# Attention of two mixers in one written TensorE order, with scaling and weight casts on GpSimd

## The chip, the cores and the metric

The kernel runs on one core of a Trainium2 chip. The metric is the device time of one execution in microseconds. The kernel before has a median of 1093.54 us in three runs (1093.34 to 1095.23).

The engines are called TensorE (PE in the rows, with PEld for its weight loads), VectorE (DVE), ScalarE (ACT), GpSimd (POOL) and SyncE (SP, which issues the loads from HBM).

## The reference

256 tokens of width 1024 go through two layers. Each layer is a half-step gated FFN, a token mixer, a second half-step FFN and a gated embedding, each with an RMS norm before and behind it. The first layer's mixer is A (8 heads in three dilation groups, mixed by their softmax denominators), the second layer's is B (16 query heads on 4 key/value heads, a band of 128 tokens to either side, a sink logit per head). All is float32.

```python
for i in range(DEPTH):
    g = norm_g[i]
    h = h + 0.5 * rms_norm(swiglu(rms_norm(h, g[0]), ffn_wi[i, 0], ffn_wo[i, 0]), g[1])
    hn = rms_norm(h, g[2])
    if mixer == 0:
        y = dilated_mixer(hn, a_wqkv[j], a_wo[j], cos, sin)
    elif mixer == 1:
        y = window_gqa_mixer(hn, b_wqkv[j], b_wo[j], b_sink[j], cos, sin)
    h = h + rms_norm(y, g[3])
    h = h + 0.5 * rms_norm(swiglu(rms_norm(h, g[4]), ffn_wi[i, 1], ffn_wo[i, 1]), g[5])
    ...
```

In both mixers the projections of h give Q, K and V; Q and K are rotated; scores are masked and turned into probabilities; these weigh V; and the output weights (`a_wo`, `b_wo`) project the result.

## The kernel before

The tokens are two tiles of 128 (`t` 0 and 1), held in `h`. Every large product is made of three passes over hi and lo halves (`PASSES`, line 34): `weight` (line 75) loads a 128x1024 tile into a buffer of `raws`, ScalarE casts the hi half (line 87), and VectorE subtracts for the lo half in two pieces (line 90). The pairs lie in `wts`, nine buffers, which the projections of a mixer, its output weights and the next FFN share.

`proj` (line 181) makes one 128x512 projection of a token tile: 24 matmuls of 512 columns into a bank of `ps_a` (two banks), with a call `mid` after the first half. `mixer_a` runs nine blocks of 512 columns (`kind` 0 is Q, 1 is K, 2 is V; `g` is the dilation group), in the order V0, V1, Q0, K0, Q1, K1, Q2, K2, V2, each for both token tiles. A Q or K block is scaled out of PSUM on ScalarE, rotated by four VectorE steps (`rope_`, lines 303 to 306), and its transposition (`heads_T`, four transposes and copies) is put off in `pend` until `flush` is called, which is the default `mid` of the next projection. `mixer_b` runs a K/V block and two Q blocks in the same manner.

Attention goes over eight units, a unit being two heads (A) or two pairs of heads (B) of one token tile: `units` has four for `t` 0, then four for `t` 1.

- `scores` makes 12 matmuls into two banks of `ps_y` (four banks), and `soft` turns each bank into probabilities: a fused mask-add and minimum on VectorE (lines 396, 543), the exponential with its sum on ScalarE (lines 397, 546), a reciprocal (398, 548) and a scaling on VectorE (399, 550). In B each bank holds two heads, so there are two of each but the reciprocal, and a copy of the sink logits (line 541).
- `trans` transposes the probabilities, 4 + 4 transposes into two banks of `ps_t` (two banks), which ScalarE copies to `w2` (line 338).
- `values` makes 16 matmuls into one bank of `ps_a` and splits the result into halves.

`attend` (line 445) goes over the units with two units of scores ahead (`AHEAD`): `score(n + 2)`, `trans(n + 1)`, `values(n)`, and after the fifth unit `finish(0)`, the output projection and norm of token tile 0 (24 matmuls of 512 columns in A, 48 in B). Behind the loop come the transposes of the new activations of tile 0 (`res[0].fin()`) and `finish(1)`; then the next FFN starts.

What sets the order: the kernel is written in program order, and a scheduler orders each engine's instructions by that order and by when it expects their inputs. `tc.manual_schedule` keeps the written order on the engines it names. Before, it encloses in the mixers only the inside of `scores` and of `values`: their matmuls keep their order, but others may come between them. DMAs of weights all go out on SP's queue in the scheduler's order.

## Time and profile before

| | |
|---|---|
| median of three runs | 1093.54 us |
| profiled execution, its own time | 1094.63 us |
| its span, first to last instruction | 1092.9 us |
| TensorE busy | 98% of the span |
| VectorE, ScalarE, GpSimd busy | 64%, 52%, 0% |
| mean granted TensorE clock | 0.99 |

Busy time counts an instruction from its start to its modelled end. TensorE's matmuls are pipelined, so a row's length is that of a run of them including the last one's end, and what a run costs is read from start to start of the rows. The idle time in brackets stands before a row, with what released it.

### The profile page before, as it was taken

Reading aid. Unit: us, or ns where it says so; the run is one execution under the profiler, and the core shown is the slowest. Engines: PE = TensorE matmul, PEld = TensorE weight load, DVE = VectorE, ACT = ScalarE, POOL = GpSimd, SP = SyncE. Lnnn points to the kernel's source line nnn. Section 1 sums busy time; section 2 is a strip of 40 time slices with the busy share of each in tenths; the row PEclk is TensorE's granted clock in tenths of the full one; section 3 lists DMA queues with packets and bytes.
Section 4 is the critical chain, followed back from the end, with each engine's and each line's share of the span. In section 5 each row is a group of like instructions: output and inputs, shape, how many; then the busy total and the mean of one; then the engine's idle time right before and its main releaser. Section 6 shows DMA issues by size and latency. Waiting matters only on the chain.

```text
span 1092.9 us, 14763 instructions
## 1 busy us (share of the span) xinstructions
PE 1066.1 (98%) x5110; PEld 862.5 (79%) x5110; DVE 694.8 (64%) x1523; ACT 570.6 (52%) x896; POOL 0.7 (0%) x6
## 2 busy tenths in 40 slices
PE   7999999999999999999999999999998999999996
PEld 6888888788877888888887888887866888888885
DVE  6765454865666855576588654655975875557465
ACT  5644343655565645454456444544675665446343
POOL 0000000000000000000000000000000000000000
PEclk8999999999999999999999999999999999999998
DMA  8865655565540575576544756655660565567601
GB/s 268 294 199 176 204 182 165 174 221 164 174 135 30 165 229 187 161 246 205 163 138 154 233 170 195 193 162 167 178 170 1 158 214 180 171 211 241 202 1 39
DMA packets 130235, 189.04 MB, mean 173 GB/s; under 512 B 9440, under 2 KB 100320, under 8 KB 130160
## 3 DMA queue, kind: packets, MB, share of 16 engines
q1 hardware_dynamic: 130160, 188.10, 54.8%
q8 instruction: 40, 0.66, 0.2%
q14 instruction: 35, 0.29, 0.1%
HBM read 187.02 MB, written 1.05 MB: 172 GB/s over the span
## 4 chain that ended last, share of the span: by engine, by line
PE 93%; DVE 3%; ACT 2%; DMA 1%; issue 1%; SPq 1%; DVEq 0%; ACTq 0%
PE psa L193 54%; PE psy L204 29%; PE pst L240 2%; PE pst L336 2%; PE psa L414 1%; PE psa L630 1%; PE psy L325 1%; PE pst L146 1%; PE psa L568 1%; PE pst L316 1%; DMA raw<-in_ffn_wi_dram 1%; ACT w L87 1%; DVE w L90 1%; PE psa L187 1%; ACT w2t L338 0%
## 5 line engine op out<-in xcount | busy, mean ns | idle before, releaser
L193 PE MATMUL psa<-w,hgT 128*128 128x512 f32 x2664 | 632.7, 393 | 0.5 <-ACT m4t L375 0.5
L193 PEld LDWEIGHTS psa<-w,hgT 128*128 128x128 f32 x2664 | 494.9, 188 | 103.3 <-ACT m4t L375 0.9
L90 DVE TENSOR_TENSOR w<-raw,w 128x512 fp32r<-128x512 f32 x672 | 435.7, 687 | 174.6 <-ACT w L87 165.1
L87 ACT CAST w<-raw 128x1024 fp32r<-128x1024 f32 (+1 forms) x340 | 352.7, 1042 | 196.2 <-issue 82.3
L204 PE MATMUL psy<-w,w2t 128*128 128x512 f32 x1056 | 260.7, 399 | 2.6 <-ACT w2t L72 2.5
L204 PEld LDWEIGHTS psy<-w,w2t 128*128 128x128 f32 x1056 | 194.4, 188 | 47.8 <-ACT w2t L72 5.4
L231 ACT ACTIVATE w2t<-psa,small 128x256 f32<-128x256 f32 x88 | 41.7, 474 | 158.8 <-PE psa L193 154.5
L232 DVE SCALAR_TENSOR_TENSOR w2t<-psa,small,w2t 128x256 f32<-128x256 f32 x88 | 42.3, 481 | 115.0 <-ACT w2t L231 115.0
L73 DVE TENSOR_TENSOR w2t<-pst,w2t 128x256 fp32r<-128x256 f32 x88 | 36.5, 415 | 9.3 <-ACT w2t L72 9.3
L72 ACT CAST w2t<-pst 128x256 fp32r<-128x256 f32 x88 | 32.1, 364 | 10.1 <-PE pst L240 10.0
L204 PE MATMUL psy<-w,m4t 128*128 128x512 f32 x144 | 37.3, 402 | 0.0
L72 ACT CAST hgT<-w2t 128x512 fp32r<-128x512 f32 x32 | 19.4, 620 | 32.2 <-DVE w2t L148 32.0
L240 PE MATMUL pst<-ident,w2t 128*128 128x128 f32 x176 | 33.5, 271 | 1.5 <-DVE w2t L232 1.5
L240 PEld LDWEIGHTS pst<-ident,w2t 128*128 128x128 f32 x176 | 24.4, 139 | 13.2 <-issue 1.8
L204 PEld LDWEIGHTS psy<-w,m4t 128*128 128x128 f32 x144 | 25.9, 188 | 6.3 <-issue 1.2
L148 DVE TENSOR_TENSOR w2t<-pst,gcol 128x512 f32<-128x512 f32 x32 | 21.2, 685 | 10.9 <-PE pst L146 10.7
L336 PE MATMUL pst<-ident,w2t 128*128 128x128 f32 x128 | 21.4, 292 | 4.4 <-DVE w2t L550 4.3
L204 PE MATMUL psy<-w,hgT 128*128 128x512 f32 x96 | 23.4, 392 | 0.0
L336 PEld LDWEIGHTS pst<-ident,w2t 128*128 128x128 f32 x128 | 14.2, 144 | 11.3 <-issue 8.2
L114 ACT ACTIVATE w2t<-psy 128x512 f32<-128x512 f32 x24 | 14.2, 593 | 16.7 <-DVE w2t L166 16.6
L171 DVE SCALAR_TENSOR_TENSOR h<-w2t,small,h 128x512 f32<-128x512 f32 x32 | 22.6, 748 | 0.4
L204 PE MATMUL psy<-m4t,hgT 128*128 128x512 f32 x96 | 22.6, 389 | 0.0
(88 smaller groups left out, 551.7 us busy)
## 6 DMA issues: line engine op xcount, KB each, us to landing
raw<-in_ffn_wi_dram SPq DMA_DIRECT2D x352, 256.0 KB, 4.1
raw<-in_ffn_wo_dram SPq DMA_DIRECT2D x88, 512.0 KB, 4.9
raw<-in_a_wqkv_dram SPq DMA_DIRECT2D x36, 512.0 KB, 4.6
raw<-in_ple_gate_dram SPq DMA_DIRECT2D x16, 512.0 KB, 3.8
raw<-in_b_wqkv_dram SPq DMA_DIRECT2D x12, 512.0 KB, 4.0
gb<-in_norm_g_dram SPq DMA_DIRECT2D x8, 512.0 KB, 4.9
raw<-in_b_wo_dram SPq DMA_DIRECT2D x16, 256.0 KB, 5.7
raw<-in_a_wo_dram SPq DMA_DIRECT2D x4, 512.0 KB, 4.7
```

The source lines that it names most:

```text
L72: nc.scalar.copy(dst_hi, src)
L73: nc.vector.tensor_tensor(dst_lo, src, dst_hi.bitcast(F32), ALU.subtract)
L87: nc.scalar.copy(w[0][:, i:i + step], raw[:, i:i + step])
L90: nc.vector.tensor_tensor(w[1][:, c], raw[:, c], w[0][:, c].bitcast(F32), ALU.subtract)
L148: nc.vector.tensor_tensor(hg, pt.rearrange("p (k q) -> p k q", k=4), gcol[:, 4 * q:4 * q + 4, self.row].unsqueeze(2).broadcast_to([P, 4, P ...
L171: nc.vector.scalar_tensor_tensor(h[t][:, s], yg[i], r, h[t][:, s], ALU.mult, ALU.add)
L193: nc.tensor.matmul(ps, lhs(a, xh, 2 * c + k), ws[c][wh][:, k * 512:(k + 1) * 512], start=(c == 0 and k == 0 and n == 0), stop=(c == 3 and ...
L204: nc.tensor.matmul(y[half], lhsf(k, xh), ws[k][wh][:, half * 512:(half + 1) * 512], start=(first and k == 0 and i == 0), stop=(last and k ...
L231: nc.scalar.activation(su[:, 0, :], ps[:, 0:256], AF.Silu, scale=acts[t].rstd)
L232: nc.vector.scalar_tensor_tensor(su[:, 1, :], ps[:, 256:512], acts[t].rstd, su[:, 0, :], ALU.mult, ALU.mult)
L240: nc.tensor.transpose(pt[:, f * P:(f + 1) * P], su[:, 1, f * P:(f + 1) * P], ident)
L336: nc.tensor.transpose(pt[:, i * P:(i + 1) * P], sm_of(a), ident)
```

## The change

TensorE's order is written out for the whole of `attend`. A function `lead` of each mixer does the last projections together with the first scores and transposes: in A, the blocks V1 and V2 are moved behind all Q and K blocks, and scores 0 to 2 and the transposes of units 0 and 1 stand between their four projections; in B, the same stands around the second Q block, with the transposes of that block's heads (`flush`) right behind its last projection. The loop then goes `values(n)`, `score(n + 3)`, (`finish(0)` after the fifth unit), `trans(n + 2)`. The hi halves of the output weights are cast by GpSimd, the scaling of the probabilities and B's copy of the sink logits go from VectorE to GpSimd, one of B's two copies of transposed probabilities goes from ScalarE to VectorE, and the pool `w2` has 14 buffers instead of 12.

```diff
--- before.py
+++ after.py
@@ -23,13 +23,13 @@
 RAWS = 5
 SPLIT_A = False
 M4 = 11
+W2 = 14
 PREP = 6
 E_AT = None
 GATE_AT = 8
 GATE_N = 4
 FA = 5
 FB = 5
-AHEAD = 2
 WARM = 9
 PASSES = ((0, 0), (0, 1), (1, 0))
 
@@ -45,7 +45,7 @@
     wts = pool("wts", 9)
     hgs = pool("hgs", 1)
     m4 = pool("m4", M4)
-    w2 = pool("w2", 12)
+    w2 = pool("w2", W2)
     ps_y = pool("ps_y", 4, space=bass.MemoryType.PSUM)
     ps_a = pool("ps_a", 2, space=bass.MemoryType.PSUM)
     ps_t = pool("ps_t", 2, space=bass.MemoryType.PSUM)
@@ -72,7 +72,7 @@
         nc.scalar.copy(dst_hi, src)
         nc.vector.tensor_tensor(dst_lo, src, dst_hi.bitcast(F32), ALU.subtract)
 
-    def weight(loads, later=False, big=False):
+    def weight(loads, later=False, big=False, pool_hi=False):
         raw = raws.tile([P, 1024], F32, name="raw", tag="raw")
         if big:
             w = [m4_tile([P, 1024], F32R) for _ in range(2)]
@@ -84,7 +84,10 @@
 
         def cast(step):
             for i in range(0, 1024, step):
-                nc.scalar.copy(w[0][:, i:i + step], raw[:, i:i + step])
+                if pool_hi:
+                    nc.gpsimd.tensor_copy(w[0][:, i:i + step], raw[:, i:i + step])
+                else:
+                    nc.scalar.copy(w[0][:, i:i + step], raw[:, i:i + step])
             for i in range(0, 1024, LO):
                 c = slice(i, i + LO)
                 nc.vector.tensor_tensor(w[1][:, c], raw[:, c], w[0][:, c].bitcast(F32), ALU.subtract)
@@ -102,8 +105,8 @@
             (lambda r, i=i: r.rearrange("p (kt f) -> p kt f", kt=2)[:, :, i * wd:(i + 1) * wd],
              v[:, :, c0:c0 + wd]) for i, c0 in enumerate(cols)], later)
 
-    def weight_rows(src, k, big=False):
-        return weight([(lambda r: r, src[k * P:(k + 1) * P, :])], big=big)
+    def weight_rows(src, k, big=False, pool_hi=False):
+        return weight([(lambda r: r, src[k * P:(k + 1) * P, :])], big=big, pool_hi=pool_hi)
 
     def inv_rms(parts, factor):
         k = 256.0 / (3.0 * factor)
@@ -330,12 +333,16 @@
     def pv_out(o_ps, oT, slot):
         split(oT[:, 0, slot, :], oT[:, 1, slot, :], o_ps[:, 0:P])
 
-    def transpose_p(sm_of, kts):
+    def transpose_p(sm_of, kts, dve=False):
         pt = bank("t")
         for i, a in enumerate(kts):
             nc.tensor.transpose(pt[:, i * P:(i + 1) * P], sm_of(a), ident)
         pT = w2_tile([P, 4, P])
-        nc.scalar.copy(pT, pt.rearrange("p (n q) -> p n q", n=4))
+        v = pt.rearrange("p (n q) -> p n q", n=4)
+        if dve:
+            nc.vector.tensor_copy(pT, v)
+        else:
+            nc.scalar.copy(pT, v)
         return pT
 
     def out_proj(t, oTs, ws, y):
@@ -396,7 +403,7 @@
             nc.vector.tensor_tensor_reduce(sm, s, msk[:, t, :], 1.0, 3e38, ALU.add, ALU.min, accum_out=mn)
             nc.scalar.activation(sm, sm, AF.Exp, scale=-1.0, bias=mn, accum_out=den)
             nc.vector.reciprocal(rd, den)
-            nc.vector.tensor_scalar(sm, sm, rd, None, ALU.mult)
+            nc.gpsimd.tensor_scalar(sm, sm, rd, None, ALU.mult)
             return sm
 
         oT, pTs = {}, {}
@@ -419,17 +426,14 @@
 
         b0 = block(2, 0)
         b0(0)
-        b1 = block(2, 1)
+        b1 = block(0, 0)
         b1(0, acts[1].fin)
         b0(1)
         b1(1)
-        for g in range(3):
-            for kind in range(2):
-                b = block(kind, g)
-                b(0)
-                b(1)
-        b = block(2, 2)
-        b(0)
+        for kind, g in ((1, 0), (0, 1), (1, 1), (0, 2), (1, 2)):
+            b = block(kind, g)
+            b(0)
+            b(1)
         sms = {}
         units = [(t, pr) for t in range(2) for pr in range(4)]
 
@@ -437,17 +441,25 @@
             if n < len(units):
                 sms[units[n]] = scores(*units[n])
 
-        b(1, lambda: score(0))
-        return attend(units, score, trans, values, 1,
-                      [lambda k=k: weight_rows(a_wo[0], k) for k in range(4)],
+        b1, b2 = block(2, 1), block(2, 2)
+
+        def lead():
+            b1(0)
+            score(0)
+            b1(1)
+            score(1)
+            b2(0)
+            trans(*units[0])
+            score(2)
+            b2(1)
+            trans(*units[1])
+
+        return attend(units, score, trans, values, lead,
+                      [lambda k=k: weight_rows(a_wo[0], k, pool_hi=True) for k in range(4)],
                       lambda t: [oT[t]], gb, row)
 
-    def attend(units, score, trans, values, done, wload, oTs, gb, row, flush=nothing):
-        ahead = AHEAD
-        for n in range(done, ahead):
-            score(n)
-        trans(*units[0])
-        res, ws = [], []
+    def attend(units, score, trans, values, lead, wload, oTs, gb, row):
+        res, ws, y0 = [], [], []
 
         def finish(t):
             if not ws:
@@ -456,15 +468,15 @@
             out_proj(t, oTs(t), ws, y)
             res.append(boundary(t, y, gb, 1.0, row))
 
-        for n, u in enumerate(units):
-            score(n + ahead)
-            if n == 0:
-                flush()
-            if n + 1 < len(units):
-                trans(*units[n + 1])
-            values(*u)
-            if n == 4:
-                finish(0)
+        with tc.manual_schedule(engines={E.PE}):
+            lead()
+            for n, u in enumerate(units):
+                values(*u)
+                score(n + 3)
+                if n == 4:
+                    finish(0)
+                if n + 2 < len(units):
+                    trans(*units[n + 2])
         res[0].fin()
         finish(1)
         return res
@@ -538,7 +550,7 @@
             mn = stat.tile([P, 2], F32, name="pair", tag="pair", bufs=12)
             den = stat.tile([P, 2], F32, name="pair", tag="pair", bufs=12)
             rd = stat.tile([P, 2], F32, name="pair", tag="pair", bufs=12)
-            nc.vector.tensor_copy(sm[:, :, 256], nsk[:, hd0:hd0 + 2])
+            nc.gpsimd.tensor_copy(sm[:, :, 256], nsk[:, hd0:hd0 + 2])
             for i in range(2):
                 nc.vector.tensor_tensor_reduce(sm[:, i, 0:256], s[:, i * 256:(i + 1) * 256], msk[:, t, 0:256], 1.0,
                                                nsk[:, hd0 + i:hd0 + i + 1], ALU.add, ALU.min,
@@ -547,14 +559,14 @@
                                      accum_out=den[:, i:i + 1])
             nc.vector.reciprocal(rd, den)
             for i in range(2):
-                nc.vector.tensor_scalar(sm[:, i, 0:256], sm[:, i, 0:256], rd[:, i:i + 1], None, ALU.mult)
+                nc.gpsimd.tensor_scalar(sm[:, i, 0:256], sm[:, i, 0:256], rd[:, i:i + 1], None, ALU.mult)
             return sm
 
         oT, pTs = {}, {}
 
         def trans(t, pr):
-            pTs[t, pr] = [transpose_p(lambda n: sm[:, n // 2, (n % 2) * P:(n % 2 + 1) * P], range(4))
-                          for sm in sms.pop((t, pr))]
+            pTs[t, pr] = [transpose_p(lambda n: sm[:, n // 2, (n % 2) * P:(n % 2 + 1) * P], range(4), u == 1)
+                          for u, sm in enumerate(sms.pop((t, pr)))]
 
         def values(t, pr):
             a, ih = pr // 2, pr % 2
@@ -578,7 +590,7 @@
             a, i = divmod(k, 4)
             r0 = (8 * a + i) * DH
             return weight([(lambda r, u=u: r[64 * u:64 * u + 64, :], b_wo[0, r0 + 256 * u:r0 + 256 * u + 64, :])
-                           for u in range(2)])
+                           for u in range(2)], pool_hi=True)
 
         b0 = kv_block()
         b0(0)
@@ -587,7 +599,6 @@
         b0(1)
         b1(1)
         b = q_block(1)
-        b(0)
         units = [(t, pr) for t in range(2) for pr in range(4)]
         sms = {}
 
@@ -597,11 +608,19 @@
 
         def mid():
             flush()
+            score(1)
+            trans(*units[0])
+
+        def lead():
+            b(0)
             score(0)
-
-        b(1, mid)
-        return attend(units, score, trans, values, 1, [lambda k=k: wo_pair(k) for k in range(8)],
-                      lambda t: [oT[t, 0], oT[t, 1]], gb, row, flush)
+            b(1, mid)
+            flush()
+            trans(*units[1])
+            score(2)
+
+        return attend(units, score, trans, values, lead, [lambda k=k: wo_pair(k) for k in range(8)],
+                      lambda t: [oT[t, 0], oT[t, 1]], gb, row)
 
     def emb_load(layer):
         pin = w2_tile([P, 2, 256])
```

## Rows read from the trace of the kernel before

**Rows 1.** Page, busy time, share of the span and instructions of each engine.

```profile
PE 1066.1 (98%) x5110; PEld 862.5 (79%) x5110; DVE 694.8 (64%) x1523; ACT 570.6 (52%) x896; POOL 0.7 (0%) x6
```

**Rows 2.** Busy by engine (instructions) in two stretches, granted clock, DMA; `start:end length` first.

```profile
308.10:356.75 48.65, 47.65 (x358) 34.71 (x358) 33.44 (x98) 31.79 (x70) 0.00 (x0) 1.00 0.20 60
800.35:865.48 65.13, 59.17 (x410) 45.08 (x409) 47.68 (x175) 43.45 (x108) 0.00 (x0) 0.95 0.23 71
```

**Rows 3.** Timeline of TensorE, projections of mixer A: start, length, line, count.

```profile
278.78 5.71 PE L193 MATMUL psa<-w,hgT 128*128 128x512 f32 x24
284.33 0.60 PE L316 MATMUL pst<-ident,w2t 128*128 128x128 f32 x4
```

**Rows 4.** Timeline of TensorE, mixer A's attention, cut groups, then whole ones.

```profile
318.79 1.09 PE L414 MATMUL psa<-w2t,m4t 128*64 128x128 f32 x14
...
321.66 0.43 PE L414 MATMUL psa<-w2t,m4t 128*64 128x128 f32 x2
...
322.65 0.66 PE L336 MATMUL pst<-ident,w2t 128*128 128x128 f32 x4
...
335.33 1.09 PE L414 MATMUL psa<-w2t,m4t 128*64 128x128 f32 x14
...
342.48 1.15 PE L325 MATMUL psy<-m4t 64*128 64x256 f32 x12
343.56 1.09 PE L336 MATMUL pst<-ident,w2t 128*128 128x128 f32 x8
344.58 1.09 PE L414 MATMUL psa<-w2t,m4t 128*64 128x128 f32 x16
```

**Rows 5.** Timeline of TensorE, mixer B's attention; in brackets idle before, and releaser.

```profile
811.12 0.68 PE L336 MATMUL pst<-ident,w2t 128*128 128x128 f32 x4 [0.36 <-DVE w2t L550]
...
814.05 1.06 PE L336 MATMUL pst<-ident,w2t 128*128 128x128 f32 x4 [1.00 <-DVE w2t L550]
...
829.24 1.12 PE L336 MATMUL pst<-ident,w2t 128*128 128x128 f32 x4
...
846.38 0.97 PE L531 MATMUL psy<-m4t 64*128 64x256 f32 x12
847.28 1.09 PE L336 MATMUL pst<-ident,w2t 128*128 128x128 f32 x8
```

**Rows 6.** Instructions by line: count | busy us, mean ns | idle before, releaser.

```profile
L90 DVE TENSOR_TENSOR w<-raw,w 128x512 fp32r<-128x512 f32 x672 | 435.7, 687 | 174.6 <-ACT w L87 165.1
L87 ACT CAST w<-raw 128x1024 fp32r<-128x1024 f32 (+1 forms) x340 | 352.7, 1042 | 196.2 <-issue 82.3 <-PE psa L193 48.0 <-ACT w2t L72 26.6
...
L338 ACT COPY w2t<-pst 128x512 f32<-128x512 f32 x32 | 18.2, 581 | 5.4 <-PE pst L336 5.4
...
L546 ACT ACTIVATE w2t<-w2t,pair 128x257 f32<-128x257 f32 x32 | 16.4, 512 | 4.4 <-DVE pair L543 4.3
L543 DVE CUSTOM_DVE_ANT_0 w2t<-psy,msk,nsk 128x256 f32<-128x256 f32 x32 | 15.1, 474 | 0.1
...
L397 ACT ACTIVATE w2t<-w2t,small 128x512 f32<-128x512 f32 x16 | 11.6, 726 | 4.3 <-DVE small L396 4.2
...
L396 DVE CUSTOM_DVE_ANT_0 w2t<-psy,msk 128x512 f32<-128x512 f32 x16 | 10.8, 674 | 0.0
...
L550 DVE TENSOR_SCALAR w2t<-w2t,pair 128x256 f32<-128x256 f32 x32 | 9.8, 351 | 0.0
...
L399 DVE TENSOR_SCALAR w2t<-w2t,small 128x512 f32<-128x512 f32 x16 | 7.7, 483 | 0.1
...
L306 DVE TENSOR_TENSOR w2t<-w2t 128x128 f32<-128x128 f32 (+1 forms) x18 | 5.1, 283 | 0.5
...
L516 ACT ACTIVATE w2t<-psa,small 128x512 f32<-128x512 f32 x4 | 2.8, 688 | 2.6 <-PE psa L193 2.6
...
L548 DVE RECIPROCAL pair<-pair 128x2 f32<-128x2 f32 x16 | 2.6, 164 | 11.6 <-ACT w2t L546 11.5
```

**Rows 7.** Instructions by line, GpSimd.

```profile
masks.py:199 POOL TENSOR_SCALAR_AFFINE_SELECT ident<-ident 128x128 f32<-128x128 f32 x1 | 0.3, 292 | 0.1
```

## Prediction

> **What bounds the kernel now.** I read the page first: TensorE is busy for 1066 of 1093 us [rows 1], so nothing can be gained except where TensorE either stands idle or takes longer over its work than the work needs. The mean hides which stages those are, so next I cut the two attention stretches out by their times: from the first scores of mixer A to the first FFN matmul behind it, and the same for mixer B [rows 2]. They last 48.65 and 65.13 us. TensorE is idle for 1.00 us of the first and 5.96 us of the second; the granted clock is 1.00 in the first and 0.95 in the second, so in the second it ran at its lower level (1.2 instead of 2.4 GHz) for about a tenth of the time, 6.5 us, which costs half of that, 3.3 us.
>
> Idle time is not the whole loss, because a busy row does not say that the order was a good one. The timeline of TensorE shows it. A projection of 24 matmuls takes 5.55 us (284.33 minus 278.78), 0.231 us each, and four transposes 0.35 us [rows 3]. Where mixer A's three attention groups stand whole, one behind the other, twelve score matmuls take 1.08 us and eight transposes 1.02 us from start to start, and sixteen value matmuls are a row of the same length as the eight transposes, so 1.02 us [rows 4]: 3.12 us for a unit (two heads of one query tile). In the steady part of the same stretch the groups are cut (two value matmuls, then four transposes, and so on), and four units take 335.33 minus 318.79, from one run of fourteen value matmuls to that of the fourth unit behind it, that is 4.14 us each [rows 4]. TensorE is fully busy there and still loses 1.02 us per unit. In mixer B whole groups take 0.90 and 1.02 us, and I take 1.02 us for the values as in A: 2.94 us for a unit; the steady part takes 829.24 minus 811.12 for three units, 6.04 us each, with idle pieces such as the 1.00 us that ended with the scaling of the probabilities on VectorE [rows 5]. So B's loop runs at the speed of the softmax chain, and A's at that of cut groups.
>
> **What whole groups would cost.** Mixer A's stretch holds half a projection (2.78), eight units (8 x 3.12 = 24.96), two output projections of 24 matmuls (48 x 0.231 = 11.1) and eight transposes of the next activations (0.7): 39.5 us, which is 9.1 under its 48.65. Mixer B's holds 2.78, four head transposes 0.35, 8 x 2.94 = 23.5, 96 x 0.231 = 22.2 and 0.7: 49.5, which is 15.6 under its 65.13. Of B's 15.6, 6.0 is idle time, 3.3 the clock and 6.3 cut groups; of A's 9.1, 1.0 is idle. 24.7 us is what a perfect written order could give, and what the new order waits for has to be taken off.
>
> **The order in mixer A, and its waits.** From `lead` on, TensorE executes as written: values(n), score(n+3), trans(n+2). Between the end of score(n+3) and trans(n+3) stand one trans, one values, one score: 3.12 us. The softmax of a unit's second head is ready after the minimum on VectorE (0.674), two exponentials (2 x 0.726), the reciprocal (0.164) and the scaling, now on GpSimd [rows 6]. GpSimd does no such operation in the trace of before. Its nearest row is the select over 128 columns of the identity matrix, 0.292 us [rows 7]; four of those for 512 columns are 1.17 us, and I take that as the upper bound, since each contains its fixed cost. The lower bound is VectorE's own 0.483 us [rows 6], as nothing suggests that GpSimd would be faster. The chain is then 2.8 to 3.5 us, and the second head's transposes come 0.51 us into the trans: no wait by itself. But ScalarE also has two copies of transposed probabilities between (2 x 0.581), which makes it up to 4.1 us after taking off the 0.51. So 0 to 1.0 us each time; I take 0.4 for five of them, 2.0 us (0 to 5). ScalarE's own work per unit, 2 x (0.726 + 0.581) = 2.6 us, fits into 3.12. By the Trainium skill, "GPSIMD Engine Reference", section 3.1, a loop over 512 elements took 769 ns; by it the sum would stay within 0.3 us of this one, and no run here shows it.
>
> The moved V projections cost nothing by themselves: the same nine weight blocks and their matmuls run, with scores 0 to 2 between them instead of after them, and a V block leaves VectorE free, having no rotation. The first two blocks, which become a V and a Q block, need one more small operation before their bank comes free: 0 to 0.3 us, taken as 0. Their DMAs on SP are reordered within one queue that brings the same bytes. Output weights: four hi halves of 1.042 us leave ScalarE for GpSimd, at 0.5 (half of ScalarE's) to 2.34 us (eight selects) each, 2 to 9 us in all, early and long before the first output projection; if that cover were gone, they would put it off by up to 2.3 us. What is next late behind a shorter loop is the next FFN, which needs h after the first output projection. Today 14.3 us pass from the end of that projection (342.48) to the FFN (356.75); in the new order 2 x 1.02 + 3 x 1.02 + 5.55 + 0.7 = 11.4 us pass. I assume that the norm fits into them; else up to 2.9 us of the gain end there. A: 9.1 - 2.0 = 7.1 us gained (4 to 9.1).
>
> **The order in mixer B, and its waits.** Here the chain is longer: minimum 0.474, four exponentials one behind the other (4 x 0.512), reciprocal 0.164, two scalings on GpSimd (each 0.351 as now on VectorE, to 0.584 as two selects) [rows 6, 7]: 3.4 to 3.9 us, less 0.51 for the second head, against 2.94 us of written work. ScalarE's copy in between adds up to 0.6 and more. I take 0.8 us of wait for trans(3), (4) and (5), 2.4 us (0 to 4.2). Score(2) is the last thing in the lead, and only values(0) and score(3) stand before trans(2): 1.92 us of cover, so 1.0 to 2.1 us, taken as 1.5. trans(0) has 2.78 + 0.35 + 0.90 = 4.0 us of cover: 0 to 1, taken as 0.5. A new wait is written into the lead: right after the last Q projection stands `flush()`, which transposes that block's heads, and every later matmul queues behind it. Those heads need the scaling out of PSUM (0.688) and four rotation steps of at most 0.283 us [rows 6]: 1.8 us, and with handoffs I take 2.0 (1.8 to 2.8). For the tail and the weights of the first output projection (three of eight have to wait for the last projection's buffers) 0.6 (0 to 1.5). That is 7.0 us of waits. With such waits the clock may fall again: it cost 3.3 us beside 6.0 us of idle time, so 0 to 3.3, taken as 2.0. Both engines that limited B fit: ScalarE 4 x 0.512 + 0.581 = 2.6 us per unit, as one of two copies and eight casts of 1.042 left it; VectorE 4 x 0.474 + at most 0.674 for the copy it gets, 2.6 us, as four scalings of 0.351 left it; GpSimd 1.4 to 2.3. B: 15.6 - 9.0 = 6.6 us gained (1.5 to 12).
>
> **The sum.** 7.1 + 6.6 = 13.7 us. The profiled execution took 1094.63 us (span 1092.9 and 1.7 around it), 1.1 us above the median of the three runs. 1094.6 - 13.7 = 1080.9, less 1.1: 1080 us.
>
> **The rivals.** *VectorE and GpSimd get in each other's way.* The lo halves of the weights are VectorE's costliest rows, 0.687 us each [rows 6]. If GpSimd's scaling has to wait out one of them per trans, the five trans in B's loop come 3.4 us later: 1083 us, and up to 1088 if A's do too. No row of before shows both engines at work. The Trainium skill, "SBUF — State Buffer", section "Who interferes with whom", states just that: a VectorE instruction with two SBUF inputs (the lo halves are such) and a GpSimd instruction that reads SBUF block each other for their whole length. That rule speaks against putting the work on GpSimd.
>
> *The written waits eat B's gain.* A strict order lets nothing else run while the flush or a late trans blocks TensorE's queue; today the scheduler fills such holes by cutting groups. If each wait is at its upper bound (2.1 + 4.2 + 1 + 2.8 + 1.5 + 3.3 = 14.9 of 15.6) and A's waits are 5, 4.8 us remain: 1089 us, with 1086 to 1094 around it. For it: B's chain is already longer than its cover. Against it: the chain gains two units of lead and a lighter ScalarE.
>
> *GpSimd becomes the bound; slower.* Per unit it gets two scalings of 512 columns in A, four of 256 in B. If 256 columns take 1.2 us, B's chain is 0.474 + 1.02 (the first head's two exponentials) + 0.164 + 4 x 1.2 = 6.5 us, less 2.94 of cover 3.5 us of wait at each of five trans, 17.5, plus 4.5 for flush, tail and clock: 22, more than the 15.6 to be had; in A two scalings of 2.4 us make a unit 4.8 us against 4.14 today, 4 us for six units. Net some 6 + 4 = 10 us slower, 1104 us. It decides from about 1.0 us per 256 columns. GpSimd's row extrapolates to 0.584, so it would have to be almost twice as slow as that.
>
> **How the numbers follow.** Forecast (1074 to 1086) 0.55; the engines in each other's way (1083 to 1088) 0.12; written waits (1086 to 1094) 0.17; GpSimd as bound (1096 and above) 0.10; waits near their lower bounds (below 1074) 0.06. 0.2% is 2.2 us, about what a measurement of this kernel can tell from no change; 1091.3 is that edge. Of the written waits about 0.06 lies above it. Faster: 0.55 + 0.12 + 0.11 + 0.06 = 0.84; same 0.06; slower 0.10. For the range, 1073 to 1092 leaves out some 0.05 below and 0.15 above.
>
> **What would show it.** Right: TensorE's timeline after shows runs of 12, 8 and 16 in the loop, A's unit period about 3.5 us and B's about 3.8, one hole of 2 us before the last head transposes in B and one before trans(2). Wrong: runs that are whole but take longer than 3.12 and 2.94 us by themselves; waits on GpSimd's scaling of over 1 us; scaling rows above 0.6 us for 256 columns; a new hole ahead of the FFN behind A. A period in A above 4 us would refute the step that the cut groups cost the time.

## The result, and the profile after

The changed kernel takes 1106.74 us (median of 4 runs, 1104.77 to 1109.10), the kernel before 1093.77 beside it: 1.0117 times as long, interval 1.0092 to 1.0142. It is slower by 13 us, outside the predicted range of 1073 to 1092, and near the 1104 us of the rival in which GpSimd becomes the bound.

Page of the changed kernel, as [rows 1]: TensorE is busy for 1.4 us less than before, and its share of the span falls. The span is 10.8 us longer (1103.7 instead of 1092.9).

```profile
PE 1064.7 (96%) x5110; PEld 864.3 (78%) x5110; DVE 690.5 (63%) x1467; ACT 555.4 (50%) x876; POOL 74.2 (7%) x82
```

To find the place I cut both executions into whole mixers, from a mixer's first 36 projection matmuls to those of the next FFN. Stretches of the kernel before, first mixer A, then B (`start:end length`, busy us of TensorE, its weight loads, VectorE, ScalarE, GpSimd, then granted clock, DMA share, GB/s):

```profile
205.34:356.75 151.41, 149.89 (x834) 118.81 (x833) 96.41 (x249) 89.80 (x148) 0.00 (x0) 1.00 0.47 148
767.35:865.48 98.13, 92.17 (x566) 72.09 (x564) 76.48 (x256) 64.00 (x144) 0.00 (x0) 0.97 0.41 111
```

The same of the changed kernel, with three parts of them:

```profile
205.22:357.10 151.88, 146.28 (x833) 119.51 (x832) 92.89 (x235) 86.21 (x144) 31.08 (x20) 0.98 0.45 144
767.56:875.42 107.86, 93.20 (x565) 73.06 (x564) 76.64 (x217) 51.36 (x127) 42.44 (x56) 0.92 0.36 96
...
320.00:340.00 20.00, 15.57 (x140) 12.21 (x138) 7.66 (x28) 11.09 (x28) 12.50 (x8) 0.83 0.17 58
...
800.00:825.00 25.00, 18.30 (x102) 13.83 (x102) 14.75 (x44) 11.08 (x28) 12.23 (x15) 0.73 0.46 133
825.00:850.00 25.00, 19.12 (x167) 13.72 (x168) 14.08 (x59) 14.30 (x50) 18.98 (x28) 0.93 0.00 1
```

A is as long as before (+0.5 us) and B is 9.7 us longer. In A TensorE's busy time falls by 3.6 us, the way that whole groups promised, but its idle time grows from 1.5 to 5.6 us; in B idle time grows from 6.0 to 14.7 us, and the clock is at its lower level for a larger part (0.92 instead of 0.97). GpSimd, idle before, works 31 and 42 us.

Which waits these are, the list of TensorE's waits tells (line, releaser: total us, times, longest):

```profile
PE pst L339 <- POOL w2t L562: 9.0, 16, 1.7
PE pst L319 <- DVE w2t L309: 5.5, 4, 2.8
PE pst L339 <- POOL w2t L406: 4.4, 4, 1.4
```

Transposes of probabilities wait for GpSimd's scaling in B (L562) and in A (L406), and transposes of heads wait, three of the four times in B, for VectorE's last rotation step (L309, which is L306 before). The same list of the kernel before has this row for the scaling on VectorE in B:

```profile
PE pst L336 <- DVE w2t L550: 4.3, 7, 1.0
```

The instructions by line and shape give the durations of GpSimd's work (count | busy us, mean ns | idle before):

```profile
L562 POOL TENSOR_SCALAR w2t<-w2t,pair 128x256 f32<-128x256 f32 x32 | 29.8, 944 | 16.2 <-DVE pair L560 14.1 <-DMA raw<-in_ffn_wi_dram 1.6
L406 POOL TENSOR_SCALAR w2t<-w2t,small 128x512 f32<-128x512 f32 x16 | 26.5, 1656 | 17.2 <-DVE small L405 17.1
L88 POOL CAST w<-raw 128x1024 fp32r<-128x1024 f32 x12 | 13.8, 1152 | 745.9 <-PE psa L196 736.8 <-DVE pair L555 4.7 <-DMA raw<-in_b_wo_dram 4.1
```

A scaling takes 0.944 and 1.656 us, against VectorE's 0.351 and 0.483 in [rows 6], and against the upper bounds of 0.584 and 1.17 that the prediction took from the select of [rows 7].

Timeline of TensorE in the changed kernel, mixer B (start, length, line, matmuls, idle before and its releaser):

```profile
806.79 0.44 PE L339 MATMUL pst<-ident,w2t 128*128 128x128 f32 x2 [1.70 <-POOL w2t L562]
...
810.39 4.78 PE L196 MATMUL psa<-w,hgT 128*128 128x512 f32 x12
817.96 1.09 PE L319 MATMUL pst<-ident,w2t 128*128 128x128 f32 x4 [2.79 <-DVE w2t L309]
...
826.35 0.44 PE L339 MATMUL pst<-ident,w2t 128*128 128x128 f32 x2 [0.51 <-POOL w2t L562]
827.25 0.44 PE L339 MATMUL pst<-ident,w2t 128*128 128x128 f32 x2 [0.47 <-POOL w2t L562]
...
829.41 1.09 PE L580 MATMUL psa<-w2t,m4t 128*64 128x128 f32 x16
```

Here is the mechanism at a glance: transposes come in pairs, one pair every 0.90 us, about the length of one scaling on GpSimd, and TensorE idles 0.46 us between them. Ahead of that the half projection takes 4.78 us instead of about 3.0, at the lower clock, and the heads' transposes wait 2.79 us. In A the same shows with the longer scaling, behind a unit that waits for nothing (same view):

```profile
318.24 1.15 PE L328 MATMUL psy<-m4t 64*128 64x256 f32 x12
...
321.36 1.15 PE L328 MATMUL psy<-m4t 64*128 64x256 f32 x12
323.93 0.65 PE L339 MATMUL pst<-ident,w2t 128*128 128x128 f32 x4 [1.43 <-POOL w2t L406]
325.77 0.81 PE L339 MATMUL pst<-ident,w2t 128*128 128x128 f32 x4 [1.18 <-POOL w2t L406]
```

### The profile page after: what moved, and what is told of

It reads as the page before. It is cut to its first block, busy times and chain, and to the rows that moved or that the text cites. A ratio compares the mean times of both kernels' runs of the same rounds, so it can differ in the third digit from the quotient of the medians.

```text
span 1103.7 us, 14799 instructions
## 1 busy us (share of the span) xinstructions
PE 1064.7 (96%) x5110; PEld 864.3 (78%) x5110; DVE 690.5 (63%) x1467; ACT 555.4 (50%) x876; POOL 74.2 (7%) x82
## 4 chain that ended last, share of the span: by engine, by line
PE 87%; DVE 5%; ACT 3%; POOL 2%; issue 1%; DMA 1%; SPq 1%; DVEq 0%; ACTq 0%; POOLq 0%
PE psa L196 52%; PE psy L207 28%; DVE w L93 2%; PE pst L243 2%; POOL w2t L562 1%; PE psa L649 1%; PE pst L339 1%; ACT w L90 1%; PE pst L319 1%; PE pst L149 1%; PE psy L328 1%; PE psa L421 1%; PE psa L190 1%; DMA raw<-in_ffn_wi_dram 1%; DMA raw<-in_ffn_wo_dram 1%
## 5 line engine op out<-in xcount | busy, mean ns | idle before, releaser
L90 ACT CAST w<-raw 128x1024 fp32r<-128x1024 f32 (+1 forms) x328 | 340.3, 1042 | 193.4 <-issue 84.0
L88 POOL CAST w<-raw 128x1024 fp32r<-128x1024 f32 x12 | 13.8, 1152 | 745.9 <-PE psa L196 736.8
L339 PE MATMUL pst<-ident,w2t 128*128 128x128 f32 x128 | 22.8, 302 | 14.2 <-POOL w2t L562 9.0
L207 PE MATMUL psy<-w,m4t 128*128 128x512 f32 x144 | 34.6, 395 | 0.0
L562 POOL TENSOR_SCALAR w2t<-w2t,pair 128x256 f32<-128x256 f32 x32 | 29.8, 944 | 16.2 <-DVE pair L560 14.1
L406 POOL TENSOR_SCALAR w2t<-w2t,small 128x512 f32<-128x512 f32 x16 | 26.5, 1656 | 17.2 <-DVE small L405 17.1
```

What stands on the lines that cost most here:

```text
L90: nc.scalar.copy(w[0][:, i:i + step], raw[:, i:i + step])
L207: nc.tensor.matmul(y[half], lhsf(k, xh), ws[k][wh][:, half * 512:(half + 1) * 512], start=(first and k == 0 and i == 0), stop=(last and k ...
L339: nc.tensor.transpose(pt[:, i * P:(i + 1) * P], sm_of(a), ident)
L406: nc.gpsimd.tensor_scalar(sm, sm, rd, None, ALU.mult)
L562: nc.gpsimd.tensor_scalar(sm[:, i, 0:256], sm[:, i, 0:256], rd[:, i:i + 1], None, ALU.mult)
```

## The experiments

Theories: **S**, the scaling on GpSimd is too long for the chain from scores to transposes; **P**, GpSimd and VectorE block each other, above all the casts and the rotation; **O**, the written order itself makes holes that the scheduler used to fill. All kernels compute the whole reference. First the result of all, each with its ratio to the kernel before that ran beside it (medians of 1092.79 to 1093.77 us), and the length of the two mixers, cut as above. The lengths come from one profiled execution of each kernel, which need not be a median one: e4's took 1111.35 us, e3's 1101.67, e6's 1096.84.

| kernel | median us | ratio to before, interval | A us | B us |
|---|---|---|---|---|
| before | 1093.77 | 1 | 151.4 | 98.1 |
| after | 1106.74 | 1.0117 (1.0092 to 1.0142) | 151.9 | 107.9 |
| e1 order alone | 1090.90 | 0.9971 (0.9959 to 0.9982) | 145.9 | 98.3 |
| e2 order + casts | 1098.83 | 1.0048 (1.0033 to 1.0063) | 146.7 | 104.2 |
| e3 order + scaling | 1103.88 | 1.0091 (1.0076 to 1.0106) | 148.0 | 105.6 |
| e4 before + scaling | 1108.86 | 1.0135 (1.0108 to 1.0162) | 158.1 | 106.4 |
| e6 before + casts | 1098.93 | 1.0046 (1.0030 to 1.0061) | 152.7 | 98.9 |
| e7 e2, casts in quarters | 1098.61 | 1.0044 (1.0029 to 1.0059) | 146.7 | 104.3 |
| e8 e1, copies on ScalarE | 1092.65 | 0.9988 (0.9979 to 0.9998) | 147.4 | 101.0 |
| e5 e1, late flush | 1086.85 | 0.9938 (0.9924 to 0.9953) | 145.9 | 93.6 |
| e9 e5, minima first in B | 1082.71 | 0.9900 (0.9885 to 0.9915) | 145.9 | 90.1 |
| e10 e9, minima first in A too | 1080.87 | 0.9882 (0.9866 to 0.9899) | 144.0 | 90.0 |
| e11 before, minima first | 1085.30 | 0.9922 (0.9907 to 0.9937) | 147.6 | 91.2 |
| e12 e10 + scaling on GpSimd | 1092.01 | 0.9989 (0.9979 to 0.9998) | 149.0 | 95.5 |

**e1: the order alone.** The changed kernel with all work of GpSimd put back.

```diff
-                if pool_hi:
-                    nc.gpsimd.tensor_copy(w[0][:, i:i + step], raw[:, i:i + step])
-                else:
-                    nc.scalar.copy(w[0][:, i:i + step], raw[:, i:i + step])
+                nc.scalar.copy(w[0][:, i:i + step], raw[:, i:i + step])
...
-            nc.gpsimd.tensor_scalar(sm, sm, rd, None, ALU.mult)
+            nc.vector.tensor_scalar(sm, sm, rd, None, ALU.mult)
...
-            nc.gpsimd.tensor_copy(sm[:, :, 256], nsk[:, hd0:hd0 + 2])
+            nc.vector.tensor_copy(sm[:, :, 256], nsk[:, hd0:hd0 + 2])
...
-                nc.gpsimd.tensor_scalar(sm[:, i, 0:256], sm[:, i, 0:256], rd[:, i:i + 1], None, ALU.mult)
+                nc.vector.tensor_scalar(sm[:, i, 0:256], sm[:, i, 0:256], rd[:, i:i + 1], None, ALU.mult)
```

> The changed kernel with GpSimd taken out again: probabilities are scaled and the sink logits copied on VectorE, hi halves of the output weights are cast on ScalarE; the written order, the 14 buffers and the copy on VectorE stay. Theory S (the scaling on GpSimd, 1.66 us per 512 and 0.94 us per 256 columns, sits in the softmax chain and undoes what the order brings): 1078 to 1088 us, as the prediction's sum had it with VectorE's own 0.483 and 0.351 us. Theory O (the written order itself costs more than it brings, by the flush and by transposes that block TensorE's queue): 1094 us or more, with the hole of 2.8 us before the last head transposes still there and B's lead as long as in the changed kernel.

Measured: 1090.90, 2.6 us faster than before, above the range of S and below that of O. A gains 5.5 us, B nothing. So the loss of the whole change, 15.8 us from here, comes with GpSimd's work; but B's gain is missing even without it. What the 14 buffers of `w2`, which stay, do by themselves wasn't tried. Timeline of TensorE in e1, mixer B:

```profile
806.06 1.09 PE L316 MATMUL pst<-ident,w2t 128*128 128x128 f32 x4 [3.34 <-DVE w2t L306]
...
811.30 1.65 PE L577 MATMUL psa<-w2t,m4t 128*64 128x128 f32 x16
...
816.88 0.67 PE L336 MATMUL pst<-ident,w2t 128*128 128x128 f32 x4 [2.12 <-DVE w2t L559]
...
821.99 1.09 PE L577 MATMUL psa<-w2t,m4t 128*64 128x128 f32 x16
...
826.50 1.09 PE L577 MATMUL psa<-w2t,m4t 128*64 128x128 f32 x16
```

The flush waits 3.34 us, the second bank's transposes 2.12, and a unit takes 826.50 minus 821.99, 4.51 us. Why, the queue of VectorE shows (same kernel, with a copy and an exponential of ScalarE):

```profile
813.12 0.17 DVE L557 RECIPROCAL pair<-pair 128x2 f32<-128x2 f32 x1 [0.82 <-ACT w2t L555]
813.20 0.47 DVE L552 CUSTOM_DVE_ANT_0 w2t<-psy,msk,nsk 128x256 f32<-128x256 f32 x1
...
814.12 0.48 DVE L552 CUSTOM_DVE_ANT_0 w2t<-psy,msk,nsk 128x256 f32<-128x256 f32 x1
...
814.80 0.59 ACT L342 COPY w2t<-pst 128x512 f32<-128x512 f32 x1 [0.43 <-PE pst L336]
815.28 0.51 ACT L555 ACTIVATE w2t<-w2t,pair 128x257 f32<-128x257 f32 x1
```

The second bank's minima (L552) stand in VectorE's queue behind the first bank's reciprocal, which idles 0.82 us for ScalarE; ScalarE then has to wait for those minima. Its own queue adds to it: the last exponential starts at 815.28, behind a copy for which ScalarE waited 0.43 us for TensorE. The chain from the end of the scores (811.3) to the transposes (816.88) is 5.6 us, not 3.4 to 3.9.

**e2 and e3: one of the two kinds of work on GpSimd.** e2 keeps the casts there, e3 the scaling and the copy of the sink logits; the diffs are the other parts of e1's.

```diff
# e2
-            nc.gpsimd.tensor_scalar(sm, sm, rd, None, ALU.mult)
+            nc.vector.tensor_scalar(sm, sm, rd, None, ALU.mult)
...
# e3
-                if pool_hi:
-                    nc.gpsimd.tensor_copy(w[0][:, i:i + step], raw[:, i:i + step])
-                else:
-                    nc.scalar.copy(w[0][:, i:i + step], raw[:, i:i + step])
+                nc.scalar.copy(w[0][:, i:i + step], raw[:, i:i + step])
```

> The changed kernel with only the scaling and the copy of the sink logits back on VectorE; the hi halves of the output weights stay on GpSimd. Theory S: within 3 us of the kernel without any GpSimd work, so 1080 to 1090 us. Theory P (GpSimd's twelve casts and VectorE's instructions with two inputs in SBUF hold each other up): 6 us or more above it, with rotation steps of about 1 us instead of 0.29 in the Q and K blocks ahead of B's attention, as in the changed kernel. Theory O: 1094 us or more, as without GpSimd.

> The changed kernel with only the hi halves of the output weights back on ScalarE; the scaling stays on GpSimd. Theory S: little is got back, 1100 to 1107 us, TensorE still waits some 9 us for GpSimd's scaling in B and 4 us in A. Theory P: most is got back, 1085 to 1095 us, and GpSimd's scaling rows become shorter as well.

Measured against e1: casts +7.9 us, scaling +13.0, both +15.8: less than the sum. S is confirmed by e3 and failed in e2, where it left the casts at most 3 us; there P came true. The casts, which the prediction had hidden behind other work, cost more than half as much as the scaling. Almost all of their price lies in B (+5.9 us; A +0.8). One way in which they act shows in the timeline of the changed kernel, VectorE first, GpSimd then:

```profile
795.28 1.04 DVE L309 TENSOR_TENSOR w2t<-w2t 128x128 f32<-128x128 f32 x1
...
795.14 1.04 POOL L88 CAST w<-raw 128x1024 fp32r<-128x1024 f32 x1 [2.71 <-DMA raw<-in_b_wo_dram]
```

The last rotation step takes 1.04 us beside a cast, where [rows 6] has 0.283, and it ends (796.32) just behind the cast (796.18). By the Trainium skill, "SBUF — State Buffer", section "Who interferes with whom", a VectorE instruction with two SBUF inputs and a GpSimd instruction that reads SBUF exclude each other; the rotation is of that kind, and these rows agree.

The other way goes through VectorE's queue. Transposes of the first unit and VectorE's rows ahead of them in e2, mixer B:

```profile
802.05 0.68 PE L339 MATMUL pst<-ident,w2t 128*128 128x128 f32 x4 [1.49 <-DVE w2t L562]
804.65 0.68 PE L339 MATMUL pst<-ident,w2t 128*128 128x128 f32 x4 [1.92 <-DVE w2t L562]
```
```profile
799.04 2.13 DVE L93 TENSOR_TENSOR w<-raw,w 128x512 fp32r<-128x512 f32 x2 [1.02 <-POOL w L88]
801.09 0.15 DVE L560 RECIPROCAL pair<-pair 128x2 f32<-128x2 f32 x1
```

The reciprocal of the softmax stands behind two lo halves, and these wait 1.02 us for GpSimd's cast of their hi half. It starts 3.7 us behind the bank's last minimum (797.38), in e1 1.2 us. So these transposes wait 1.49 and 1.92 us, in e1 only the second, for 1.04. By them e2's mixer B falls 2.5 us further behind e1's; its waits for the rotation ahead of them are 1.4 us (0.54 and 0.82), and the half projection behind them, at the lower clock, takes 4.58 us instead of 2.99. How much is the rotation's and how much the queue's, no run separates.

**e4 and e6: the same alone, without the order.** The kernel before with only its scaling (e4) or only its casts of output weights (e6) on GpSimd.

```diff
# e4
-            nc.vector.tensor_scalar(sm, sm, rd, None, ALU.mult)
+            nc.gpsimd.tensor_scalar(sm, sm, rd, None, ALU.mult)
...
-                nc.vector.tensor_scalar(sm[:, i, 0:256], sm[:, i, 0:256], rd[:, i:i + 1], None, ALU.mult)
+                nc.gpsimd.tensor_scalar(sm[:, i, 0:256], sm[:, i, 0:256], rd[:, i:i + 1], None, ALU.mult)
# e6
-                nc.scalar.copy(w[0][:, i:i + step], raw[:, i:i + step])
+                if pool_hi:
+                    nc.gpsimd.tensor_copy(w[0][:, i:i + step], raw[:, i:i + step])
+                else:
+                    nc.scalar.copy(w[0][:, i:i + step], raw[:, i:i + step])
```

> The kernel before, with nothing changed but the scaling of the probabilities, which goes to GpSimd; the scheduler's order and the casts on ScalarE stay. Theory S: slower than before by 5 to 20 us, since the chain that B's loop runs at today has VectorE's scaling in it, and 0.6 us per piece are added to it. Theory O or P alone: within 3 us of the kernel before, as neither the written order nor the casts are in it.

> The kernel before, with nothing changed but the twelve hi halves of the output weights, which GpSimd casts. Theory P (a GpSimd cast and a VectorE instruction with two inputs in SBUF hold each other up, whatever the order): rotation steps beside casts take about 1 us instead of 0.29, as in the changed kernel; the time is 3 to 9 us above the kernel before if TensorE waits for them. Rival (the casts cost only where the written order has no slack, here the scheduler fills the holes): within 2 us of the kernel before, though the long rows are there.

Measured: scaling +15.3 us, casts +5.3. Neither edit needs the written order to cost what it costs. In e6 the rotation step at 788.77 takes 1.06 us too; but its A and B are longer than before by only 2.1 us in all, and where the rest of the 5.3 lies no trace shows. e4 has a surprise: from 820 to 842 us TensorE does not wait at all. A stretch of three units of e4's mixer B (columns as above), and the transposes that begin the first and the second of them:

```profile
820.35:841.92 21.57, 21.57 (x111) 14.59 (x109) 8.86 (x44) 11.23 (x37) 11.48 (x13) 0.50 0.02 7
```
```profile
820.35 1.12 PE L336 MATMUL pst<-ident,w2t 128*128 128x128 f32 x4
...
827.54 1.12 PE L336 MATMUL pst<-ident,w2t 128*128 128x128 f32 x4
```

TensorE is busy all of the time, at a granted clock of 0.50, its lower level of 1.2 GHz, and a unit takes 7.19 us. Ahead of it stand waits on GpSimd of 0.5 to 1.5 us. So here the price stands in the clock, which stayed down though no further wait followed; that the waits ahead brought it down is argued, not tried. GpSimd itself is busy for 11.5 of these 21.6 us and bounds nothing there.

**e7: casts in quarters.** e2, with each cast as four of 256 columns. If a long lock is the harm, shorter ones should give some of it back.

```diff
+            if pool_hi:
+                step = 256
```

> The written order with the casts on GpSimd and the scaling on VectorE (1098.8 us), each cast now four pieces of 256 columns instead of one of 1024. Theory P, with a hold for the length of one instruction: a rotation step waits for a quarter of a cast at most, some 0.3 us instead of up to 0.8, and half or more of the 8 us that the casts cost come back: 1091 to 1095 us. Rival (the pair is held while GpSimd has such work, or the lateness is that of the weights and not of the rotation): 1097 to 1101 us.

Measured: 1098.61 against e2's 1098.83, no gain, as the rival had it. GpSimd's row by line, and the first and the last of four rotation steps of VectorE in e7:

```profile
L90 POOL CAST w<-raw 128x256 fp32r<-128x256 f32 x48 | 25.4, 576 | 783.0 <-DVE w L95 476.7 <-PE psa L198 293.5 <-issue 12.8
```
```profile
790.78 0.41 DVE L308 TENSOR_TENSOR w2t<-w2t,rp 128x64 f32<-128x64 f32 x1
...
791.98 0.37 DVE L311 TENSOR_TENSOR w2t<-w2t 128x128 f32<-128x128 f32 x1
```

Instead of one step of 1.04 us there are four of about 0.4, and the 48 casts take 25.4 us in place of the 14.2 of e2's twelve. The reciprocal behind the lo halves still starts 3.3 us after the last minimum. The harm is spread, not lessened: my expectation that half would come back was wrong.

**e8: the copies.** e1 with both copies of transposed probabilities of B on ScalarE again, the part of the change that e1 keeps.

```diff
-            pTs[t, pr] = [transpose_p(lambda n: sm[:, n // 2, (n % 2) * P:(n % 2 + 1) * P], range(4), u == 1)
+            pTs[t, pr] = [transpose_p(lambda n: sm[:, n // 2, (n % 2) * P:(n % 2 + 1) * P], range(4))
```

> The written order without GpSimd work (1090.9 us), with both of B's copies of transposed probabilities on ScalarE as before. It tells what the move of one copy to VectorE does by itself. If ScalarE bounds B's loop, a unit takes longer than the 4.50 us of the written order, by up to the copy's 0.58, 2 to 4 us in all: 1093 to 1095 us. If VectorE bounds it, the copy's 0.69 us on VectorE is the longer one, and the time falls to 1087 to 1090 us.

Measured: 1092.65, 1.8 us above e1; the two intervals just overlap. B is 2.7 us longer. A part of that is the clock (0.92 in B, in e1 0.97), but at the full clock too a unit takes 4.99 us (values at 824.22 and 829.21) instead of 4.51. Giving VectorE one copy was right.

**e5: the flush later.** e1 with the transposes of B's last heads put off until score(3) is out, and score(2) ahead of trans(1).

```diff
+            if n == 3:
+                flush()
...
-            flush()
-            trans(*units[1])
             score(2)
+            trans(*units[1])
```

> The written order without GpSimd work (1090.9 us), with one more change in mixer B: the transposes of the last Q block's heads come behind score(3) instead of right behind the block's last projection, and score(2) comes ahead of trans(1). Theory F (B's loss in the lead is the flush that blocks TensorE's queue: a hole of 3.34 us, and behind it the lower clock from 806 to 813 us, which costs another 3 us): 1083 to 1087 us, no hole of over 1.5 us before the head transposes, granted clock at 1.00 behind them. Theory C (the softmax chain is the floor there too, and the hole moves to trans(1) and trans(2)): 1089 to 1092 us.

Measured: 1086.85, B 4.8 us shorter than in e1. The hole of 3.34 us is gone: it was the written order's own, as O had it. Waits on the scaling remain (7.4 us in six, the longest 2.25).

**e9 and e10: minima first.** e5 with the softmax written step by step over both banks: all minima, then all exponentials, then reciprocals and scalings; in B (e9), and in A as well (e10).

```diff
-            return [soft(t, x, 8 * a + 4 * u + 2 * ih) for u, x in enumerate(s)]
+            gens = [soft(t, x, 8 * a + 4 * u + 2 * ih) for u, x in enumerate(s)]
+            for step in range(3):
+                done = [next(g) for g in gens]
+            return done
...
+            yield
```

> The written order without GpSimd work and with the late flush (1086.9 us), with one more change in mixer B: the softmax of a unit's two banks is written step by step (four minima, then four exponentials, then reciprocals and scalings) instead of bank by bank. Theory Q (what makes B's chain 5.6 us long where the sum had 3.4 to 3.9 is VectorE's queue: the second bank's minima stand behind the first bank's reciprocal, which waits for ScalarE): the chain falls to some 4 us, B's unit period from 4.50 to 3.4 to 3.8 us, four to five units gain about 0.9 us each: 1081 to 1084 us. Rival (the length is that of the operations, and the order of the queue only spreads it): 1085.5 to 1088 us, period 4.3 us or more.

> The same as the run with B's minima first, and the same in mixer A as well (both minima, both exponentials, then reciprocals and scalings). Theory Q: A's remaining holes (0.86, 1.21 and 0.64 us in front of transposes) go, 1 to 3 us less than with B's alone. Rival: A's holes come from the two copies on ScalarE between the exponentials, and stay: within 1 us of B's alone.

Measured: 1082.71 and 1080.87; e10 is the quickest of all kernels here, 12 us under the kernel before. TensorE in e10, mixer B, the values of the first and the last of four units and the waits of the second:

```profile
808.18 1.09 PE L588 MATMUL psa<-w2t,m4t 128*64 128x128 f32 x16
...
811.03 0.68 PE L336 MATMUL pst<-ident,w2t 128*128 128x128 f32 x4 [0.84 <-DVE w2t L570]
811.95 0.67 PE L336 MATMUL pst<-ident,w2t 128*128 128x128 f32 x4 [0.24 <-DVE w2t L570]
...
821.09 1.09 PE L588 MATMUL psa<-w2t,m4t 128*64 128x128 f32 x16
```

The wait of 2.12 us in e1 is 0.24 to 0.84 here, and a unit takes (821.09 - 808.18) / 3 = 4.3 us. I had expected 3.4 to 3.8, the rival 4.3 or more: the time came as forecast, the unit did not, and the chain still ends last. Of the 3.5 us that B gains over e5, 1.5 lie in the first unit (6.61 us there, 806.34 to 812.95; here 5.13, 803.05 to 808.18). In A the units take 3.36 to 3.46 us.

**e11: minima first without the written order.** The kernel before with the step-by-step softmax alone, the same edit as e10's.

```diff
-            return [soft(t, x) for x in s]
+            gens = [soft(t, x) for x in s]
+            for step in range(3):
+                done = [next(g) for g in gens]
+            return done
...
+            yield
```

> The kernel before in the scheduler's own order, with the softmax of both mixers written step by step as in the other two runs; no written TensorE order, no late flush, nothing on GpSimd. If the queue on VectorE was all that held B's loop, this alone brings B's unit from 6.04 us to under 5 and the kernel to 1085 to 1090 us. If the written order is needed for it (whole groups, two units of lead), within 3 us of the kernel before.

Measured: 1085.30, A 3.8 us and B 6.9 us shorter than before. TensorE's idle time in B falls from 6.0 to 2.4 us, so most of it was VectorE's queue, not the order of TensorE. On the same chip the written order, with the late flush, VectorE's copy and the 14 buffers, adds another 4.4 us (e10), 3.6 of them in A.

**e12: scaling on GpSimd in the best order.** e10 with that one edit.

```diff
-            nc.vector.tensor_scalar(sm, sm, rd, None, ALU.mult)
+            nc.gpsimd.tensor_scalar(sm, sm, rd, None, ALU.mult)
...
-                nc.vector.tensor_scalar(sm[:, i, 0:256], sm[:, i, 0:256], rd[:, i:i + 1], None, ALU.mult)
+                nc.gpsimd.tensor_scalar(sm[:, i, 0:256], sm[:, i, 0:256], rd[:, i:i + 1], None, ALU.mult)
```

> The quickest kernel so far (written order, late flush, minima first in both parts, casts on ScalarE: 1080.9 us) with one thing put back, the scaling of the probabilities on GpSimd. Theory, scaling is on the chain in any order: each pair of transposes of the second part waits for scalings of 0.92 us that follow one another on one engine, and the first part's for 1.56 us; the gap between this kernel and the quickest is then near the 13 us that the same edit cost on the written order as given: 1089 to 1096, second-part period 4.8 us or more, waits of TensorE on line 562 of several us. Rival, the 13 us came from the softmax's queue and not from the scaling's length: with minima first the chain has room, the scaling is hidden and VectorE is relieved of 14 us of work; 1078 to 1084, period 4.2 to 4.4 as without it.

Measured: 1092.01, 11.1 us above e10 (10.3 between the spans: A +5.0, B +5.5). The theory holds, the rival falls: even with the queue mended the scaling's length is on the path. A part of B's price is again the clock (0.96, in e10 1.00). TensorE's waits in e12, and its timeline in B:

```profile
PE pst L336 <- POOL w2t L570: 5.3, 11, 1.0
PE pst L336 <- POOL w2t L408: 4.0, 4, 1.4
```
```profile
822.50 0.44 PE L336 MATMUL pst<-ident,w2t 128*128 128x128 f32 x2 [0.99 <-POOL w2t L570]
823.41 0.44 PE L336 MATMUL pst<-ident,w2t 128*128 128x128 f32 x2 [0.47 <-POOL w2t L570]
```

The pairs of transposes are again 0.91 us apart.

## Why the prediction was wrong

**The step that failed: the cost of GpSimd's scaling.** I took 0.584 us for 256 columns and 1.17 for 512 as upper bounds, as two and four selects, "since each contains its fixed cost". Measured are 0.944 and 1.656 (the shortest 0.920 and 1.562). Between the two shortest lie 0.642 us for 256 columns, 2.5 ns each; on that line 128 columns would be 0.60 us, an estimate, twice the select. A row of another operation was an estimate, not a bound, and no end of the range should have stood on it. The figure of the Trainium skill that the prediction weighed ("GPSIMD Engine Reference", section 3.1, 769 ns for 512 elements, given as the best case of a loop) lies lower still; the measured 1562 decides.

But the scaling is not the whole miss. From the forecast of 1080 it is 10.9 us to the order without GpSimd's work (e1), most of them in B; another 13.0 come with the scaling (e3), and 2.9 more with the casts besides.

The prediction's own rival saw the loss: it wanted "about 1.0 us per 256 columns" to decide, 0.94 were there, and its 1104 us came within 3 us. That it came so near is in part luck. It reckoned with 1.2 and 2.4 us, with a slower A and without a price of the casts; with the scaling alone (e3) A is 3.4 us shorter than before and B 7.5 longer. I gave it 0.10 because the price had to be "almost twice" the select's, and 0.944 is 1.6 times 0.584. Two of the signs of being wrong that it named came: scaling rows above 0.6 us for 256 columns, and a wait on the scaling of over 1 us (1.7).

**The casts: right duration, wrong cover.** 1.152 us lies inside 0.5 to 2.34, and I hid all of it behind other work. But the harm is not when they end; it is what they do on VectorE in the meantime. They stretch the rotation, on which the head transposes of mixer B hang, and they hold up the lo halves, which stand ahead of the first softmax in VectorE's queue. e2 minus e1 makes it 7.9 us, e6 alone 5.3. The rival of the two engines in each other's way was priced only for the scaling, at the lo halves; the casts were left out.

**Whole groups: right.** In the changed kernel the groups are whole, runs of 12, 8 and 16, and where nothing waits A's unit is 321.36 - 318.24 = 3.12 us, as computed. A's order was to give 7.1 us: e1 gave 5.5. The 7.4 of e10 have the minima first in them, which alone gave 3.8 (e11).

**B's chain, mis-sized.** I forecast waits of 7.0 us and a lower clock of 2.0, leaving 6.6. Without GpSimd's work (e1) nothing was left. The flush cost 3.34 instead of 2.0, and the chain was 5.6 instead of 3.4 to 3.9, since I lined up four exponentials behind one minimum and did not read VectorE's in-order queue. The flush hangs on the same queue: e1's four rotation steps, 1.0 us of work, are spread from 803.82 to 805.91 among scalings and lo halves. With both mended (e9, e10) B gains 8.1, and A and B together 15.5 us, the whole kernel 11.9. That is near the 13.7 of the sum, but with edits that the sum did not have.

**The clock.** It was expected to cost B 2.0 us and A nothing. By the two stretches of B with a lower clock shown above it cost up to 8.5 (0.27 x 25 + 0.07 x 25), where the prediction read 3.3 before; this is an estimate, too high by whatever part of that time TensorE was idle. The clock fell in A as well: 0.83 from 320 to 340 us, where e3, with the same scaling but without the casts, has rows of 1.09 us for the values instead of 1.98 and a mixer A 3.9 us shorter. What tipped it there wasn't tried and stays open; so does why casts and scaling add up to more than their sum in A (+6.0 against 0.8 and 2.1) and to less in B (+9.5 against 5.9 and 7.2). That the clock can differ behind equal waits, e8 shows. Its mixer A has the code of e1's, and TensorE waits 0.86 and 1.21 us there as in e1; but then the values take 1.98 us in e8 and 1.09 in e1, and A is 1.5 us longer:

```profile
324.27 0.92 PE L336 MATMUL pst<-ident,w2t 128*128 128x128 f32 x4 [1.21 <-DVE w2t L403]
325.12 1.98 PE L418 MATMUL psa<-w2t,m4t 128*64 128x128 f32 x16
```

So a difference of this size between single executions can be the clock's alone.

**Right besides:** the FFN behind A follows the end of the first output projection after 11.4 us in e1 (340.63 to 352.02) and 11.5 in the changed kernel (345.60 to 357.10), with no new hole, as forecast.

## What to carry to other kernels

An upper bound for an operation that an engine has not done in the trace must not come from another kind of operation: carry the forecast at two and three times that price, and let that case have its chance when the operation stands on the chain. Before TensorE's order is rewritten, read the in-order queue of the engine that feeds it: here the order of a softmax's minima on VectorE was worth 7.5 us by itself. Work given to an idle engine is not free for the busy ones: look which instructions of the others slow down beside it, which stand in a queue behind what it delivers, and what waits for those.

## What the hardware showed that I had not expected

- GpSimd takes 2.5 ns per column for a scaling by a value per partition, but 1.04 us for a cast of 1024 columns, 1.0 ns each, no longer than ScalarE's 1.042 us in [rows 6].
- Beside a cast on GpSimd a VectorE step of 0.29 us took 1.04; cutting the casts into quarters made them longer (25.4 us in sum instead of 14.2) and the kernel no faster.
- TensorE stayed at a granted clock of 0.50 through 21.57 us in which it was busy all the time (e4, one execution), after a few waits of 0.5 to 1.5 us: a unit at that level took 7.19 us, longer than the 6.04 with waits before [rows 5].
